# A short-convolution layer in a four-layer backbone step: its weight-pair pool opens earlier, and its last loads are cut by columns

## The chip, the cores and the metric

The kernel runs on one core of a Trainium2 chip. The metric is the device time of one execution in microseconds (us); the times given are medians over runs on the chip. The core has five engines that run side by side, each with its own queue of instructions: PE (TensorE, matrix products), DVE (VectorE), ACT (ScalarE), POOL (GpSimd) and SP (SyncE, which here issues all DMA loads and stores). An engine takes its instructions strictly in order: an instruction that waits holds everything behind it.

## The reference

Four layers work on 640 tokens (512 of a sample, 128 of a prompt) with 1024 channels. Each is `x <- LayerNorm(ALPHA * x + gate * Mixer(x * (1 + scale) + shift))`; shift, scale and gate are computed per layer from a condition vector. The mixers are an HGRN2 recurrence (layer 0), the short convolution (layer 1), an RG-LRU (layer 2) and latent attention (layer 3). The change is in layer 1:

```python
def short_conv_mixer(h, w_in, conv_w, conv_b, w_out):
    bg, cg, v, g = jnp.split(h @ w_in, 4, axis=-1)
    z = depthwise_conv(cg * v, conv_w, conv_b, (SC_KERNEL // 2, SC_KERNEL // 2))
    return (jax.nn.silu(g) * bg * z) @ w_out
x = layer_norm(DEEPNORM_ALPHA * x + gate * out, ln_g[l], ln_b[l])
```

## The kernel before

**Precision.** Each product is made of three: both operands are split into a high part (`wh`, `xh`: a cast) and a low part (`wl`, `xl`: the operand minus its high part), and high by high, high by low and low by high are summed in PSUM. For a weight tile this means a load by SP (`wraw`, 512 KB, L76), a cast on ACT (L80) and a subtraction on DVE (L82). There are three raw buffers and four pairs of split ones (pool `wp`, NW = 4).

**The convolution layer.** `sconv` (L902) computes, for each of eight blocks j of 128 channels, the four products of `h @ w_in`, the three taps of the convolution on ACT and DVE, and the gated result `o`. Block 0 is computed plainly: `mpair` (L265) makes cg and v, `mtile` (L179) makes bg and then g. Blocks 1 to 7 use a scheme with seven half-size products in place of eight: `_prep_pair` (L85) loads two weight blocks at once (`praw`, 1 MB, L93), forms sums of their quarters on DVE in place (L108), and splits each into high and low: `wab` and `s24` into pool `wp`, `wd` and `s13` (`wdh`, `wdl`, `wsh`, `wsl`) into the pool `self.sw`, where `praw` lives as well. Casts are on ACT (L102), low parts on DVE (L105). `spair` (L199) then runs the seven products on PE (L214) into three PSUM banks `psx`, `psy`, `psz`; between products that use the same bank again ACT copies it out (`keep`, L217 to L221). Its other operand, sums of token halves `t1` to `t4` in the pool `tp`, is made once by `token_sums` (L244). `next_w` (L145) prepares weights ahead; a pair is only prepared if `self.sw` exists (L150). Before the change `self.sw` is opened at L916, after `mpair` of block 0 and after `self.zctx.close()` (L914), which frees the tile z that layer 0's output still uses.

**The output projection.** `outproj` (L426) multiplies `o` by `w_out` in three passes over columns: 0 to 255, 256 to 511, 512 to 1023; within a pass it takes five tiles i of 128 tokens. The product of a tile goes to a PSUM bank `pso` (four banks for five tiles; L175 to L177). DVE then frees the bank by `t1 = pso * gateb` (L447), and adds `ALPHA * z` (L453), where z is the layer's input. In layer 1 z comes back from DRAM as the normalised input without scale and offset, so DVE first applies `lng` and `lnb` to the pass's columns (L451):

```python
if l == 1:
    for v, op in ((self.lng, ALU.mult), (self.lnb, ALU.add)):
        nc.vector.tensor_tensor(out=z[:, i, c0:c0 + cw], in0=z[:, i, c0:c0 + cw], in1=v[:, c0:c0 + cw], op=op)
```

z, `lng` and `lnb` are loaded in `build` (L1529 to L1533), the two gate rows (sample and prompt, broadcast over partitions) in `load_bcast` (L390): five loads of z, then `lng`, `lnb`, two gates, 512 KB each. The order of the instructions on each engine is set by a scheduler that estimates times; the program text gives priorities and the order among equals.

Of the kernel before, what the change touches and what calls it, by code (L numbers as in the profile page):

```python
# [9 lines left out]
F32 = mybir.dt.float32  # L10
# [6 lines left out]
P = 128  # L17
D = 1024
# [6 lines left out]
NT = T // P  # L25
# [25 lines left out]
class Kernel:  # L51
# [337 lines left out]

    def load_bcast(self, l):  # L390
        nc, I = self.nc, self.I
        self.gateb = []
        for s in range(2):
            g = self.bp.tile([P, D], F32, name=f"gateb{l}_{s}", tag=f"gateb{s}")
            nc.sync.dma_start(out=g, in_=self.gate_dram[l][s, :].partition_broadcast(P))
            self.gateb.append(g)
        if l == self.NL - 1:
            self.load_affine(l)

# [500 lines left out]
    def sconv(self):  # L900
        nc, tc = self.nc, self.tc
        with ExitStack() as ctx:  # L902
            sp = ctx.enter_context(tc.tile_pool(name="sp", bufs=1))
            for j in range(KT):
                self.rate = 0.0 if j == 0 else 0.45
                if j == 0:
                    cg = sp.tile([P, T], F32, name="ca0", tag="ca0")
                    p = cg
                    pss = self.mpair()
                    for hf in range(2):  # L910
                        c = SPL[hf]
                        nc.scalar.copy(out=cg[:, c], in_=pss[hf][:, 0])
                        nc.vector.tensor_tensor(out=p[:, c], in0=cg[:, c], in1=pss[hf][:, 1], op=ALU.mult)
                    self.zctx.close()  # L914
                    tp = ctx.enter_context(tc.tile_pool(name="tp", bufs=1))
                    self.sw = ctx.enter_context(tc.tile_pool(name="sw", bufs=2))  # L916
                    with tc.high_priority():
                        self.token_sums(tp)
                else:
                    p, v = self.spair(sp, 0)  # L920
                    nc.vector.tensor_tensor(out=p, in0=p, in1=v, op=ALU.mult)
                zz = sp.tile([P, T], F32, name="zz", tag="zz")

                def cw(i):
                    return self.v("sc_conv_w", i * KT + j, 1)
                nc.scalar.activation(out=zz, in_=p, func=AF.Identity, scale=cw(1), bias=self.v("sc_conv_b", j, 1))
                self.taps(zz, p, (-1, 1), (cw(0), cw(2)))
                th = sp.tile([P, T], F32, name="th", tag="th")
                if j == 0:
                    bg = sp.tile([P, T], F32, name="ca1", tag="ca1")  # L930
                    g = sp.tile([P, T], F32, name="cb0", tag="cb")
                    ps = self.mtile()
                    nc.vector.tensor_tensor(out=self.hv(bg), in0=self.hv(zz), in1=ps, op=ALU.mult)
                    ps = self.mtile()
                    nc.scalar.activation(out=self.hv(th), in_=ps, func=AF.Tanh, scale=0.5)
                    nc.vector.scalar_tensor_tensor(out=self.hv(g), in0=self.hv(th), scalar=1.0, in1=ps, op0=ALU.add,
                                                   op1=ALU.mult)
                    nc.vector.scalar_tensor_tensor(out=self.o[:, j, :], in0=g, scalar=0.5, in1=bg, op0=ALU.mult,
                                                   op1=ALU.mult)
                    continue  # L940
                if j == KT - 1:
                    self.split_o(slice(0, 4), slice(0, HALF))
                bg, g = self.spair(sp, 1)
                if j == KT - 1:
                    self.split_o(slice(4, 7), slice(0, HALF))
                for c in (slice(0, HALF), slice(HALF, T)) if j == KT - 1 else (slice(0, T),):
                    nc.vector.tensor_tensor(out=bg[:, c], in0=zz[:, c], in1=bg[:, c], op=ALU.mult)
                    nc.scalar.activation(out=th[:, c], in_=g[:, c], func=AF.Tanh, scale=0.5)
                    nc.vector.scalar_tensor_tensor(out=g[:, c], in0=th[:, c], scalar=1.0, in1=g[:, c], op0=ALU.add,
                                                   op1=ALU.mult)  # L950
                    nc.vector.scalar_tensor_tensor(out=self.o[:, j, c], in0=g[:, c], scalar=0.5, in1=bg[:, c],
                                                   op0=ALU.mult, op1=ALU.mult)
                    if j == KT - 1:
                        self.split_o(slice(7, 8), c)
                        if c.start == 0:
                            self.split_o(slice(0, 7), slice(HALF, T))
            self.sw = None
# [544 lines left out]
    def build(self):  # L1502
        nc, tc, ctx = self.nc, self.tc, self.ctx
        self.setup()
        self.open_x()
        self.o = self.cp.tile([P, KT, T], F32, name="o")
        self.zdram = self.dp.tile([NT, P, D], F32, name="zdram")
        self.zctx = ExitStack()
        wlist = weight_list(self.NL)
        self.weights(wlist)  # L1510
        self.credit, self.rate = -2.0, 0.0
        self.sw = None
        self.pend = None
        self.adaq, self.adafin = [], []
        self.start()
        for l in range(self.NL):
            if l == 0:
                self.adaq = self.ada_units(0, (2,)) + (self.ada_units(1) if self.NL > 1 else [])
            elif l + 1 < self.NL:
                self.adaq = self.ada_units(l + 1)  # L1520
            self.rate = (0.45, 0.4, 0.6, 0.0)[l]
            if l == 0:
                self.hgrn()
                self.open_z()
                for i in range(NT):
                    nc.sync.dma_start(out=self.z[:, i, :], in_=self.I["x_sample"][i * P:(i + 1) * P, :] if i < 4
                                      else self.I["x_prompt"])
            elif l == 1:
                self.sconv()  # L1529
                self.open_z()  # L1530
                for i in range(NT):
                    nc.sync.dma_start(out=self.z[:, i, :], in_=self.zdram[i])
                self.load_affine(0)  # L1533
            elif l == 2:
                self.rglru()
            else:
                self.actx.close()
                self.mla()
                for i in range(NT):
                    nc.sync.dma_start(out=self.z[:, i, :], in_=self.zdram[i])  # L1540
            with ExitStack() as c2:
                self.bp = c2.enter_context(tc.tile_pool(name=f"bp{l}", bufs=1))
                self.load_bcast(l)
                if l + 1 < self.NL:
                    self.flush_ada()
                    self.coeffs(l + 1)
                self.outproj(l)
        self.zctx.close()
        self.close_x()
        self.actx.close()  # L1550
# [127 lines left out]
```

## Time and profile before

| | |
|---|---|
| median of 3 runs | 1472.36 us (1470.63 to 1477.81) |
| the profiled execution | 1473.87 us, of which the instructions span 1472.1 us |
| PE busy | 1416.0 us (96% of the span) |
| DVE, ACT busy | 1085.2 us (74%), 751.0 us (51%) |
| mean granted TensorE clock | 0.99 |
| layer 0's output projection, PE | 447.4 to 507.3 us |
| first products of layer 1's block 0 | from 507.3 us |
| layer 1's output projection, PE | from 732.3 us |

The profile is of one execution. Busy time is what an engine's instructions took; the waits list says how long an engine stood idle and what ended the wait. Start times are microseconds from the start of the span.

### The profile page before, as it was taken

How to read it: one execution, taken by the hardware profiler on the slowest of the kernel's cores; microseconds unless marked ns; L12 is line 12 of the kernel's file. 1: busy time of each engine (PE TensorE's matmuls, PEld its weight loads, DVE VectorE, ACT ScalarE, POOL GpSimd, SP SyncE). 2: the span in 40 equal slices, each digit the busy share in tenths (PEclk: the TensorE clock that was granted, in tenths of full speed). 3: DMA queues.
4: the chain of work that ended last, by engine and by line, in shares of the span. 5: the costliest groups of instructions: out<-in, count | busy, mean ns of one | idle time of the engine just before them, and what ended most of it. 6: DMA issues, size and time to landing. Idle time of an engine off the chain costs nothing.

```text
span 1472.1 us, 26193 instructions
## 1 busy us (share of the span) xinstructions
PE 1416.0 (96%) x10570; PEld 1299.0 (88%) x10570; DVE 1085.2 (74%) x1987; ACT 751.0 (51%) x1350; POOL 86.0 (6%) x194
## 2 busy tenths in 40 slices
PE   6999999999999989999999999999999999999997
PEld 4898989989989889999988989899899888888795
DVE  4777677477567688888787799786656868677777
ACT  2656456356443545455416577622643467566630
POOL 0000000000000100000001011110110200000002
PEclk9999999999999999999999999999999999999999
DMA  9322324223325344443253433443123200001041
GB/s 349 113 80 72 110 80 163 81 90 118 105 84 196 127 142 133 154 145 142 96 207 103 125 128 130 154 145 111 47 78 105 79 19 17 24 30 30 29 144 72
DMA packets 48920, 160.48 MB, mean 109 GB/s; under 512 B 5840, under 2 KB 11040, under 8 KB 47008
## 3 DMA queue, kind: packets, MB, share of 16 engines
q1 hardware_dynamic: 48800, 158.82, 31.9%
q8 instruction: 83, 1.36, 0.4%
q14 instruction: 37, 0.30, 0.1%
HBM read 149.69 MB, written 9.10 MB: 108 GB/s over the span
## 4 chain that ended last, share of the span: by engine, by line
PE 71%; DVE 14%; ACT 8%; DMA 3%; issue 3%; POOL 1%; SPq 0%; POOLq 0%; DVEq 0%; ACTq 0%
PE psmm L195 14%; PE psx L214 7%; PE pso L175 4%; PE pso L177 4%; PE pso L176 4%; PE psz L214 3%; PE poa L1427 3%; PE psmm L1058 2%; DVE wl L82 2%; PE ptp L1414 2%; PE psA L350 2%; PE psy L214 2%; DVE tr L1088 1%; PE psS L175 1%; PE psS L177 1%
## 5 line engine op out<-in xcount | busy, mean ns | idle before, releaser
L80 ACT CAST wh<-wraw 128x1024 fp32r<-128x1024 f32 (+4 forms) x129 | 127.2, 997 | 124.5 <-PE pso L177 68.3
L195 PE MATMUL psmm<-xh,wh 128*128 128x320 f32 x784 | 186.3, 316 | 2.2 <-ACT vt L707 1.7
L195 PE MATMUL psmm<-xh,wl 128*128 128x320 f32 x784 | 181.5, 311 | 0.0
L195 PE MATMUL psmm<-xl,wh 128*128 128x320 f32 x784 | 180.8, 311 | 0.0
L82 DVE TENSOR_TENSOR wl<-wraw,wh 128x1024 fp32r<-128x1024 f32 (+4 forms) x129 | 147.9, 1158 | 28.6 <-ACT wh L80 28.2
L175 PE MATMUL pso<-wh,xh 128*128 128x256 f32 (+1 forms) x464 | 150.2, 325 | 3.4 <-DVE t L447 3.3
L176 PE MATMUL pso<-wl,xh 128*128 128x256 f32 (+1 forms) x464 | 149.3, 322 | 0.0
L177 PE MATMUL pso<-wh,xl 128*128 128x256 f32 (+1 forms) x464 | 149.2, 322 | 0.0
L195 PEld LDWEIGHTS psmm<-xh,wh 128*128 128x128 f32 x784 | 130.9, 189 | 9.9 <-issue 3.5
L195 PEld LDWEIGHTS psmm<-xl,wh 128*128 128x128 f32 x784 | 131.1, 188 | 2.6 <-issue 2.0
L195 PEld LDWEIGHTS psmm<-xh,wl 128*128 128x128 f32 x784 | 131.8, 188 | 0.7 <-issue 0.6
L175 PEld LDWEIGHTS pso<-wh,xh 128*128 128x128 f32 x464 | 87.9, 190 | 10.9 <-DVE t L447 3.5
L177 PEld LDWEIGHTS pso<-wh,xl 128*128 128x128 f32 x464 | 88.0, 190 | 7.3
L176 PEld LDWEIGHTS pso<-wl,xh 128*128 128x128 f32 x464 | 88.2, 190 | 6.6
L1398 ACT ACTIVATE pe<-psS,mx 128x768 f32<-128x768 f32 (+1 forms) x80 | 63.7, 797 | 38.8 <-DVE mx L1396 38.4
L1396 DVE TENSOR_REDUCE mx<-psS 128x1 f32<-128x768 f32 (+1 forms) x80 | 65.3, 817 | 7.8 <-PE psS L177 7.1
L1414 PE MATMUL ptp<-ident,pe 128*128 128x128 f32 x400 | 56.8, 273 | 0.8 <-ACT pe L1398 0.8
L447 DVE TENSOR_TENSOR t<-pso,gateb 128x256 f32<-128x256 f32 (+1 forms) x58 | 29.2, 510 | 31.3 <-PE pso L177 30.1
L177 PE MATMUL psmm<-xh,wl 128*128 128x384 f32 (+1 forms) x160 | 49.4, 308 | 1.1 <-DVE wl L82 1.1
L176 PE MATMUL psmm<-xl,wh 128*128 128x384 f32 (+1 forms) x160 | 49.9, 312 | 0.3 <-DVE xl L166 0.3
L175 PE MATMUL psmm<-xh,wh 128*128 128x384 f32 (+1 forms) x160 | 49.8, 311 | 0.0
L1427 PE MATMUL poa<-pT,v 128*64 128x256 f32 (+1 forms) x416 | 48.8, 377 | 0.7 <-ACT pT L1416 0.4
(497 smaller groups left out, 3786.1 us busy)
## 6 DMA issues: line engine op xcount, KB each, us to landing
wraw<-in_wpack SPq DMA_DIRECT2D x109, 512.0 KB
araw<-in_ada_rest SPq DMA_DIRECT2D x80, 512.0 KB
praw<-in_wpack SPq DMA_DIRECT2D x14, 1024.0 KB
araw<-in_ada_first SPq DMA_DIRECT2D x16, 512.0 KB
zdram<-z SPq DMA_DIRECT2D x10, 512.0 KB
z<-zdram SPq DMA_DIRECT2D x10, 512.0 KB
gateb<-gate_dram SPq DMA_DIRECT2D x8, 512.0 KB
wraw<-in_wpack SPq DMA_DIRECT2D x8, 320.0 KB
```

The lines of the kernel that those rows point to most:

```text
L80: self.tc.keep_in_program_order(nc.scalar.copy(out=wh[:, :n], in_=raw[:, :n]))
L82: nc.vector.tensor_tensor(out=wl[:, :n], in0=raw[:, :n], in1=wh[:, :n].bitcast(F32), op=ALU.subtract)
L175: nc.tensor.matmul(ps, lhsT=ah, rhs=bh, start=(i == 0), stop=False)
L176: nc.tensor.matmul(ps, lhsT=ah, rhs=bl, start=False, stop=False)
L177: nc.tensor.matmul(ps, lhsT=al, rhs=bh, start=False, stop=(i == n - 1))
L195: nc.tensor.matmul(ps[hf][:, :HALF], lhsT=w[:, k, :], rhs=x[:, k, hf * HALF:(hf + 1) * HALF], start=(first and k == 0), stop=(last and k = ...
L214: nc.tensor.matmul(ps, lhsT=u[:, k, :], rhs=v[:, k, :], start=(first and st and k == 0), stop=(en and k == 3), skip_group_check=True)
L350: nc.tensor.matmul(ps[32 * j:32 * j + 32, :], lhsT=self.csil[:, k, :], rhs=raw[:, j * 256:(j + 1) * 256], start=(k == 2 * u), stop=(k == 2 ...
L1396: nc.vector.reduce_max(out=mx, in_=ps[:, :nk], axis=AX.X, negate=True)
L1398: nc.scalar.activation(out=pe[:, :nk], in_=ps[:, :nk], func=AF.Exp, bias=mx[:, 0:1], accum_out=g["sm"][:, n, hp:hp + 1])
L1414: nc.tensor.transpose(pt[:, kk, :], pe[:, (k0 + kk) * P:(k0 + kk + 1) * P], self.ident)
L1427: nc.tensor.matmul(po[hp * 64:(hp + 1) * 64, 0, :nq], lhsT=v4[:, kt, vc + hp * 64:vc + (hp + 1) * 64], rhs=g["pt"][hp][:, kk, :nq], start= ...
```

## The change

Two edits. In `sconv` the pool `self.sw` is opened together with `sp`, before block 0, and no longer after `tp`. At the end of layer 1, z, `lng`, `lnb` and the gates are loaded by the columns of the three passes: eighteen loads of 128 KB to 768 KB in place of nine of 512 KB, all in `load_bcast` now. The bytes are the same.

```diff
     def load_bcast(self, l):
         nc, I = self.nc, self.I
-        self.gateb = []
-        for s in range(2):
-            g = self.bp.tile([P, D], F32, name=f"gateb{l}_{s}", tag=f"gateb{s}")
-            nc.sync.dma_start(out=g, in_=self.gate_dram[l][s, :].partition_broadcast(P))
-            self.gateb.append(g)
+        self.gateb = [self.bp.tile([P, D], F32, name=f"gateb{l}_{s}", tag=f"gateb{s}") for s in range(2)]
+        for c in (slice(0, 256), slice(256, 512), slice(512, D)) if l == 1 else (slice(0, D),):
+            if l == 1:
+                nc.sync.dma_start(out=self.z[:, 0:2, c], in_=self.zdram[0:2, :, c].rearrange("i p n -> p i n"))
+                if c.start == 0:
+                    self.lng = self.zp.tile([P, D], F32, name="lng0", tag="lng")
+                    self.lnb = self.zp.tile([P, D], F32, name="lnb0", tag="lnb")
+                nc.sync.dma_start(out=self.lng[:, c], in_=I["ln_g"][0, c].partition_broadcast(P))
+                nc.sync.dma_start(out=self.lnb[:, c], in_=I["ln_b"][0, c].partition_broadcast(P))
+            for s in range(2):
+                nc.sync.dma_start(out=self.gateb[s][:, c], in_=self.gate_dram[l][s, c].partition_broadcast(P))
+                if l == 1 and s == 0:
+                    nc.sync.dma_start(out=self.z[:, 2:NT, c], in_=self.zdram[2:NT, :, c].rearrange("i p n -> p i n"))
         if l == self.NL - 1:
             self.load_affine(l)
...
     def sconv(self):
...
             sp = ctx.enter_context(tc.tile_pool(name="sp", bufs=1))
+            self.sw = ctx.enter_context(tc.tile_pool(name="sw", bufs=2))
             for j in range(KT):
...
                     self.zctx.close()
                     tp = ctx.enter_context(tc.tile_pool(name="tp", bufs=1))
-                    self.sw = ctx.enter_context(tc.tile_pool(name="sw", bufs=2))
...
             elif l == 1:
                 self.sconv()
                 self.open_z()
-                for i in range(NT):
-                    nc.sync.dma_start(out=self.z[:, i, :], in_=self.zdram[i])
-                self.load_affine(0)
```

The changed file is longer, so the same statement has a higher line number in it: L447, L451, L453, L455 become L456, L460, L462, L464, and L913 becomes L923. A number behind a name is a buffer; `pso_1_3` is the third index of the second pass, token tile 3.

**Place 1, layer 0's output projection, second pass.** SP's queue before; `wraw_5244` to `wraw_5407` are the four weight tiles of the third pass, `wraw_5413` and `wraw_5419` those of `mpair`:

```order
L76 DMA wraw_5244<-in_wpack 128x1024
L344 DMA arows_6132<-in_ada_b 1x256 x2
L76 DMA wraw_5250<-in_wpack 128x1024
L76 DMA wraw_5401<-in_wpack 128x1024
L344 DMA arows_6132<-in_ada_b 1x256
L76 DMA wraw_5407<-in_wpack 128x1024
L344 DMA arows_6132<-in_ada_b 1x256
L76 DMA wraw_5413<-in_wpack 128x1024
```

And now:

```order
L76 DMA wraw_5244<-in_wpack 128x1024
L93 DMA praw_5871<-in_wpack 128x2048
L76 DMA wraw_5250<-in_wpack 128x1024
L76 DMA wraw_5401<-in_wpack 128x1024
L76 DMA wraw_5407<-in_wpack 128x1024
L93 DMA praw_5998<-in_wpack 128x2048
L76 DMA wraw_5413<-in_wpack 128x1024
```

The first two pair loads stand here now; before they stood sixteen rows further down, behind all five of layer 0's stores of z. On DVE the work of both pairs comes along as far as it needs no `wp` buffer. Before, from the end of the same pass:

```order
L455 BN_STATS stats_5086<-z 128x6
L82 TENSOR_TENSOR wl_5403<-wraw_5401,wh_5402 128x1024
L447 TENSOR_TENSOR t_5397<-pso_1_4_5372,gateb_1_5042 128x256
L82 TENSOR_TENSOR wl_5409<-wraw_5407,wh_5408 128x1024
L453 SCALAR_TENSOR_TENSOR z<-z,t_5397 128x256
```

And now (the second pair, `praw_5998`; the first pair's four stand further up in the same way):

```order
L105 TENSOR_TENSOR wdl_6003<-praw_5998,wdh_6002 128x512
L456 TENSOR_TENSOR t_5368<-pso_1_3_5343,gateb_0_5040 128x256
L108 TENSOR_TENSOR praw_5998<-praw_5998 128x512
L462 SCALAR_TENSOR_TENSOR z<-z,t_5368 128x256
L108 TENSOR_TENSOR praw_5998<-praw_5998 128x512
L464 BN_STATS stats_5086<-z 128x6
L82 TENSOR_TENSOR wl_5403<-wraw_5401,wh_5402 128x1024
L105 TENSOR_TENSOR wsl_6005<-praw_5998,wsh_6004 128x1024
L82 TENSOR_TENSOR wl_5409<-wraw_5407,wh_5408 128x1024
L456 TENSOR_TENSOR t_5397<-pso_1_4_5372,gateb_1_5041 128x256
```

Four pieces per pair (`wdl`, two sums, `wsl`) have moved here; one of them stands between two low parts that the third pass needs.

**Place 2, the start of layer 1.** DVE before, from the first low part of a pair on:

```order
L105 TENSOR_TENSOR wl_5874<-praw_5871,wh_5873 128x1024
L105 TENSOR_TENSOR wdl_5876<-praw_5871,wdh_5875 128x512
L105 TENSOR_TENSOR wdl_6003<-praw_5998,wdh_6002 128x512
L166 TENSOR_TENSOR t2l<-o,t2h 128x1280
L108 TENSOR_TENSOR praw_5871<-praw_5871 128x512
L108 TENSOR_TENSOR praw_5998<-praw_5998 128x512
L108 TENSOR_TENSOR praw_5871<-praw_5871 128x512
L108 TENSOR_TENSOR praw_5998<-praw_5998 128x512
L166 TENSOR_TENSOR t3l<-o,t3h 128x1280
L261 SCALAR_TENSOR_TENSOR o<-o 128x4x320
```

And now:

```order
L105 TENSOR_TENSOR wl_5874<-praw_5871,wh_5873 128x1024
L166 TENSOR_TENSOR t3l<-o,t3h 128x1280
L166 TENSOR_TENSOR t2l<-o,t2h 128x1280
L108 TENSOR_TENSOR praw_5871<-praw_5871 128x512
L261 SCALAR_TENSOR_TENSOR o<-o 128x4x320
L108 TENSOR_TENSOR praw_5871<-praw_5871 128x512
L923 TENSOR_TENSOR ca_5700<-ca_5700,psmm 128x256
L166 TENSOR_TENSOR t4l<-o,t4h 128x1280
```

On PE the second `mtile` of block 0 (`psmm`, 48 products) stood behind the products of `psy` and `psz` with pair weights; now it stands ahead of most of them, and the first pair's products follow one another like this:

```order
L214 MATMUL psx<-xh,wl_5874 128x320
L214 MATMUL psz<-t1h,wsl_5878 128x320
L214 MATMUL psz<-t1h,wsh_5877 128x320
L214 MATMUL psz<-t1l,wsh_5877 128x320
L214 MATMUL psz<-t1h,wsl_5878 128x320
L350 MATMUL psA_0_0_6134<-araw_0_0_6135,csil 32x256
L214 MATMUL psx<-t2h,wh_5879 128x320
```

Only these five stand between the end of one product in `psx` and the next one in it.

**Place 3, the start of layer 1's output projection.** DVE before, `wl_8077` being the second low part of the first pass:

```order
L166 TENSOR_TENSOR xl<-o,xh 128x320
L82 TENSOR_TENSOR wl_8077<-wraw_8075,wh_8076 128x1024
L82 TENSOR_TENSOR wl_8083<-wraw_8081,wh_8082 128x1024
L82 TENSOR_TENSOR wl_8089<-wraw_8087,wh_8088 128x1024
L451 TENSOR_TENSOR z<-z,lng_8053 128x256 x5
L451 TENSOR_TENSOR z<-z,lnb_8055 128x256 x5
L447 TENSOR_TENSOR t_8118<-pso_0_0_8093,gateb_0_8060 128x256
```

And now:

```order
L166 TENSOR_TENSOR xl<-o,xh 128x320
L460 TENSOR_TENSOR z<-z,lng_8054 128x256 x2
L82 TENSOR_TENSOR wl_8086<-wraw_8084,wh_8085 128x1024
L82 TENSOR_TENSOR wl_8092<-wraw_8090,wh_8091 128x1024
L82 TENSOR_TENSOR wl_8098<-wraw_8096,wh_8097 128x1024
L456 TENSOR_TENSOR t_8127<-pso_0_0_8102,gateb_0_8051 128x256
L460 TENSOR_TENSOR z<-z,lnb_8055 128x256
```

The first `t` has come up to directly behind the three low parts, but two products with `lng` now stand ahead of them.

## Rows read from the trace of the kernel before

**Rows 1.** The page, busy time of each engine, share and instructions.
```profile
PE 1416.0 (96%) x10570; PEld 1299.0 (88%) x10570; DVE 1085.2 (74%) x1987; ACT 751.0 (51%) x1350; POOL 86.0 (6%) x194
```

**Rows 2.** PE's waits: what it waited for, us, times, longest.
```profile
PE psy L214 <- ACT wh L102: 3.8, 1, 3.8
...
PE pso L175 <- DVE t L447: 3.3, 1, 3.3
```

**Rows 3.** Windows at the first wait: PE busy (instructions), clock, DMA share, GB/s.
```profile
533.04:536.80 3.76, 0.00 (x0) 0.89 0.78 264
536.80:542.72 5.92, 5.92 (x21) 0.50 0.28 68
```

**Rows 4.** Windows at the second wait, columns as in Rows 3.
```profile
744.07:747.51 3.44, 0.16 (x2) 1.00 1.02 416
747.51:751.03 3.52, 3.52 (x17) 0.52 0.72 291
```

**Rows 5.** Chain of waits from 505 to 560 us: start, us, what.
```profile
515.01 7.15 DMA praw<-in_wpack
...
528.68 2.41 DVE praw L108 x4
531.09 1.40 DVE t3l L166
...
533.93 1.26 ACT t4h L163
535.19 1.57 ACT wh L102 x3
...
544.40 7.04 PE psmm L195 x48
```

**Rows 6.** Windows: PE, PEld, DVE, ACT, POOL busy, clock, DMA share, GB/s.
```profile
462.00:477.00 15.00, 15.00 (x124) 14.82 (x124) 10.02 (x21) 3.00 (x3) 0.00 (x0) 1.00 0.39 137
515.00:541.00 26.00, 21.90 (x152) 20.62 (x151) 25.04 (x30) 14.19 (x23) 0.00 (x0) 0.90 0.45 162
```

**Rows 7.** DVE's timeline from 735 us: start, us, what [idle before, releaser].
```profile
736.30 3.50 DVE L82 TENSOR_TENSOR wl<-wraw,wh 128x1024 fp32r<-128x1024 f32 x3 [0.46 <-ACT wh L80]
743.13 1.77 DVE L451 TENSOR_TENSOR z<-z,lng 128x256 f32<-128x256 f32 x5 [3.33 <-DMA lng<-in_ln_g]
745.36 1.77 DVE L451 TENSOR_TENSOR z<-z,lnb 128x256 f32<-128x256 f32 x5 [0.46 <-DMA lnb<-in_ln_b]
```

**Rows 8.** SP's timeline at 732 us: issues of z's loads.
```profile
732.50 2.26 SPq L1532 DMA_DIRECT2D z<-zdram  x5
```

**Rows 9.** DVE's and PE's timelines at the start of layer 1.
```profile
523.77 1.22 DVE L105 TENSOR_TENSOR wl<-praw,wh 128x1024 fp32r<-128x1024 f32 x1
...
529.82 0.31 PE L214 MATMUL psy<-xh,wh 128*128 128x320 f32 x1
```

**Rows 10.** Timelines of PE and ACT: a bank's last product and its copy.
```profile
715.07 0.31 PE L214 MATMUL psx<-t3h,wsl 128*128 128x320 f32 x1
715.47 0.43 ACT L220 COPY u<-psx 128x320 f32<-128x320 f32 x1 [1.39 <-PE psx L214]
```

**Rows 11.** Tile praw: durations in ns, least, median, most; first and last start.
```profile
L105 DVE TENSOR_TENSOR wsl<-praw,wsh x14: 1214/1218/1220, 536.8 to 711.2; 128x1024 fp32r<-128x1024 f32 x14
```

**Rows 12.** Timelines of SP, DVE and PE in layer 0's output projection.
```profile
460.64 1.82 SPq L76 DMA_DIRECT2D wraw<-in_wpack  x2
465.91 1.22 DVE L82 TENSOR_TENSOR wl<-wraw,wh 128x1024 fp32r<-128x1024 f32 x1 [0.75 <-ACT wh L80]
477.24 1.21 DVE L82 TENSOR_TENSOR wl<-wraw,wh 128x1024 fp32r<-128x1024 f32 x1
477.30 0.40 PE L175 MATMUL pso<-wh,xh 128*128 128x512 f32 x1
```

**Rows 13.** Timelines of SP and ACT: a weight load's issue and its first use.
```profile
453.20 1.30 SPq L76 DMA_DIRECT2D wraw<-in_wpack  x3
456.81 1.05 ACT L80 CAST wh<-wraw 128x1024 fp32r<-128x1024 f32 x1 [4.04 <-DMA wraw<-in_wpack]
```

## The prediction

> **What bounds the kernel now.** I read the page first: PE is busy for 1416.0 us, 96% of the span, so the end moves only by what PE stands idle or runs slowly [rows 1]. Next come PE's waits. In the part of the program that the change touches there are two, one each: 3.8 us in `psy`, for a cast of a pair's weights, and 3.3 us in `pso`, for DVE's `t` [rows 2].
>
> Then the clock around each, because a wait can cost more than its length. After the first, PE works from 536.80 to 542.72 at a granted clock of 0.50, which is 1.2 GHz in place of 2.4: 21 products take 5.92 us [rows 3]. The second leaves 3.52 us at 0.52 [rows 4]. Before both, PE had been idle for over three microseconds. The Trainium skill's page "TensorE: Matmul & The Clock Gate", section "Part 1: The HAM clock gate", describes this fall to half rate, but advises leaving its ramp out of a model, since it is below one percent of a typical span.
>
> Then who is late. At the first wait the chain runs from the load of the first two pairs, issued only at 515.01, over DVE's sums and ACT's `t4h` to three casts at 535.19 [rows 5]. DVE is busy for 25.04 of the 26 us from 515 to 541, PE for 21.90 [rows 6]. DVE is full here; in the second and third pass of layer 0's output before it (462 to 477) it has 15 - 10.02 = 5.0 us free, and ACT 12 us.
>
> At the second wait DVE stands idle for 3.33 us until `lng` lands at 743.1, multiplies five tiles, waits again for `lnb` and adds five more; only then, at about 745.4 + 1.7 = 747.1, comes the first `t`, which frees the bank that PE wants [rows 7]. The first load of z was issued at 732.50 [rows 8]. DMA moved 416 GB/s at the end of this stretch [rows 4]: the loads are limited by their bytes, and DVE waits for columns that the first pass does not need.
>
> **The change part by part.** *First wait, what goes.* Idle 3.77 us (533.03 to 536.80), and of the 5.92 us at half clock 0.50 x 5.92 = 2.96 us: together 6.7 us. Two things remove it. The second `mtile`, 7.04 us of PE work [rows 5], now stands ahead of the products that wait, and that alone is more than 3.77. And DVE's two `wdl` and four sums have left the chain: six times 2.41/4 = 0.60, that is 3.6 us [rows 5], of which one sum comes back in front of `o` (0.6).
>
> What could be late next: `mtile` needs a PSUM bank that `ca` (now L923) frees. From the low part at 523.77 DVE now takes this (1.22), three pieces of 1280 columns (1.40 each), two sums (0.60) and `ca`, a fifth of such a piece (0.28) [rows 5, 9]: 523.77 + 6.9 = 530.7. PE came to `psy` at 529.82 [rows 9] and does eight products at 7.04/48 = 0.147 first, so it asks at 531.0. A margin of 0.3 us: bounds 0 and 1 us (the error of so many terms), and I take 0.
>
> *The copies of* `psx`. Five products now stand between two uses of the bank, 5 x 0.147 = 0.7 us. A bank's last product starts at 715.07, its copy ends at 715.90: 0.83, less 0.15 for the product itself, 0.7 us [rows 10]. If a weight cast of 1.57/3 = 0.52 stands ahead of the copy on ACT, PE waits about 0.5; one does ahead of the first. Bounds 0 and three times 0.5; I take 0.4.
>
> *Layer 0's output.* Per pair `wdl` and two sums (0.60 each) and `wsl`, 1.22 [rows 11], come in: 6.0 us for both, against 5.0 free, so something slides by about 1 us. The banks cover `t`. The tight place is the low part that began at 477.24 and ended at 478.45, ahead of which a `wsl` (1.22) has been put, while a `t` of 256 columns (0.28 by its size) went behind. PE uses that low part 12 products after 477.30; a product of 320 columns takes 0.147 (the 48 of `mtile`), one of 512 thus 0.235, so at 480.1 [rows 5, 12]: of 1.65 us 0.7 are left. Bounds 0 and 0.7; I take 0. ACT's six casts (3.1 us) fit into 12 us. The pair loads add 2.1 MB to SP's queue; at 416 GB/s 2.5 us each, in a stretch that moves 137 GB/s [rows 6].
>
> *Second wait, what goes.* 3.28 us idle and 0.48 x 3.52 = 1.69 at low clock [rows 4]: 5.0 us. Now the first `t` needs only the first pass's columns.
>
> *Second wait, what comes.* Two products with `lng` stand ahead of the low part that PE needs at once. A 512 KB load was issued at 453.20 and used at 456.81 [rows 13]: 3.6 us, of which 1.26 are bytes at 416 GB/s, so about 2.35 are fixed. The first z piece and `lng`, 384 KB, issued at 732.50 and 0.45 later, land at 732.95 + 2.35 + 0.9 = 736.2. The two products take 2 x 1.77/5 = 0.7, the low parts start at 736.9 in place of 736.30: 0.6 late [rows 7, 8]. Bounds 0 and, if the pieces arrive as late as the whole tile did (743.1), 7.5; the fixed part of rows 13 is nearest, and I take 0.5. The first `t` then comes at 736.9 + 3.5 = 740.4, where PE asks at 744.07 + 0.5: 4 us of margin.
>
> *Sum.* 6.7 + 5.0 - 0.4 - 0.5 = 10.8 us less. The profiled execution took 1473.87, 1.5 above the median, so 1463.1 for it; for the median 1472.36 - 10.8 = 1461.6. By the page's advice, with the waits alone, it would be 7.05 - 0.9 = 6.2 us less, 1466.2.
>
> **The rivals.** *One wait comes back in another place.* At the end: `lng` lands 3 us or more late and DVE holds the low parts, which no PSUM banks cushion; PE then waits as long as before and loses the clock again. Gain 6.7 - 0.4 = 6.3, 1466.1. At the start: the `ca` chain or a copy is late by 3 us; gain 5.0 - 0.5 = 4.5, 1467.9. For it: DVE's order is strict, the margins are 0.3 and nothing. Against: half of DVE's excess has gone, and the loads are the same kind as before.
>
> *The clock's part is not given back.* PE waits less, but small waits remain in both places and it still runs them at 1.2 GHz: 1466.2. Against: both falls came within one idle stretch of over 3 us, and those stretches go. [...]
>
> *Slower: SP is held.* The first `praw` load now stands ahead of three weight tiles of layer 0's third pass. If its memory is not free when SP reaches it, those tiles wait behind it. The next tile was issued at 460.64, its low part ended at 467.1 and PE used it at 477.30 [rows 12]: 10.2 us of cover. PE stalls by the time beyond 470.8, and the kernel is slower once the hold passes 470.8 + 10.8 = 481.6. Held as long as in the old pool, to 515.01 [rows 5], it would be 44 us of stall: 1472 - 11 + 44 = 1505. For it: that load did go out as late as 515.01. Against: the pool is now opened below what layer 0 still uses, and its first load no longer stands behind the stores of z.
>
> *No change.* Both waits go, and other waits of the same size appear behind them: 1472. DVE, full from 515 on, would have to stay late.
>
> **How the numbers follow.** Forecast 0.70; one wait back 0.14; clock not given back 0.05; no change 0.07; slower 0.04. The forecast's own range is 1459 to 1465: the unknown costs at zero (11.7 less) and the lowest run, 1.7 below the median, at one end; at the other 3.4 us of them more. For 8 in 10 the range takes in the cases up to 1468: 1459 to 1468. A measurement of this kernel can tell about 0.5%, 7.4 us, from no change: faster means below 1465.0. That is the forecast, 0.70; within 0.5% lie one wait back, the clock and no change, 0.26; slower 0.04.
>
> **What would show it.** In the changed kernel's profile the two lines of PE's waits are gone, and PE's granted clock is 1.00 from 505 to 770 us. DVE's `wsl` of the first two pairs stand before 480 us. `lng` lands within 4 us of z's first issue, and the first `t` of layer 1 comes before PE has filled four banks. It is wrong if PE waits over 1 us for `wl` at the first pass, for `ca` or a copy at the second `mtile` and the first pair, or if SP issues the third pass's weights of layer 0 later than 470 us.

## The result and the profile after

The changed kernel takes 1464.11 us (median of 5 runs, 1461.02 to 1465.82) against 1474.52 for the kernel before in the same comparison: a ratio of 0.9929, interval [0.9913, 0.9946], or 10.4 us less. The forecast was 1461.6, 10.8 us less. Most of what is left between 1461.6 and 1464.11 is the base: the forecast stood on a median of 1472.36, and more runs of the kernel before gave 1474.5 to 1475.2.

PE's waits in the changed kernel, from 447 us to 832 (the whole of what the change touches):

```profile
PE psA L350 <- DMA araw<-in_ada_rest: 1.2, 2, 1.0
PE pso L176 <- DVE wl L82: 1.1, 1, 1.1
PE psmm L176 <- DVE xl L166: 0.3, 1, 0.3
```

Both rows of [rows 2] are gone. `psA` and `psmm` waited before too (1.4 and 0.3 us there). New is 1.1 us for `wl`. The clock, in windows (columns as in Rows 6):

```profile
505.00:770.00 265.00, 263.45 (x1893) 249.40 (x1892) 217.13 (x349) 124.03 (x225) 3.43 (x7) 1.00 0.42 146
```

PE is busy for 263.45 of 265 us, at 1.00 all the way; before, two stretches of it ran at half clock [rows 3, 4].

Where the time came from is read by stage, between first products of the output projections. The tile `pso` before, in layer 0's (first row) and layer 1's projection, with first and last start at the end of the times:

```profile
L175 PE MATMUL pso<-wh,xh x120: 277/284/483, 447.4 to 505.8; 128*128 128x256 f32 x80, 128*128 128x512 f32 x40
L177 PE MATMUL pso<-wh,xl x120: 277/285/415, 732.5 to 796.5; 128*128 128x256 f32 x80, 128*128 128x512 f32 x40
```

And in the changed kernel:

```profile
L175 PE MATMUL pso<-wh,xh x120: 277/285/482, 450.1 to 508.5; 128*128 128x256 f32 x80, 128*128 128x512 f32 x40
L177 PE MATMUL pso<-wh,xl x120: 277/285/396, 728.3 to 788.5; 128*128 128x256 f32 x80, 128*128 128x512 f32 x40
```

The first products of L175 in layer 1 started at 732.3 and 728.0. So three stages, in us:

| stage | before | after | difference |
|---|---|---|---|
| start of the program to layer 0's output projection | 447.4 | 450.1 | +2.7 |
| from there to layer 1's output projection (first wait) | 284.9 | 277.9 | -7.0 |
| layer 1's output projection, first to last product (second wait) | 64.3 | 60.5 | -3.8 |
| the whole span | 1472.1 | 1463.9 | -8.2 |

The rest of the span differs by 0.1. The first stage holds the same instructions in both kernels; its 2.7 us are scatter between executions: added up from the clock in the traces, PE stood at half clock for 13.7 us of it before and for 20.5 us after (last section). The two stages that the change touches give 10.8 us.

The places that the forecast named, in the changed kernel. SP's queue in layer 0's output projection:

```profile
456.75 0.33 SPq L93 DMA_DIRECT2D praw<-in_wpack  x1
463.36 3.59 SPq L76 DMA_DIRECT2D wraw<-in_wpack  x3
```

The first pair load left at 456.75, and the weight tiles behind it at 463.36, 2.7 later than before [rows 12], which is the 2.7 of the first stage: SP was not held. DVE there and at the start of layer 1:

```profile
471.39 1.22 DVE L105 TENSOR_TENSOR wsl<-praw,wsh 128x1024 fp32r<-128x1024 f32 x1
...
479.66 1.22 DVE L105 TENSOR_TENSOR wsl<-praw,wsh 128x1024 fp32r<-128x1024 f32 x1
...
533.03 0.42 DVE L923 TENSOR_TENSOR ca<-ca,psmm 128x256 f32<-128x256 f32 x1
```

And PE's chain of work at that second place:

```profile
525.66 7.04 PE psmm L195 x48
532.70 1.17 PE psy L214 x8
533.87 7.04 PE psmm L195 x48
```

The second `mtile` started at 533.87 without a wait; `ca`, which frees its bank, had ended at 533.45. The start of layer 1's output projection, in the timelines of SP and DVE:

```profile
728.22 0.39 SPq L396 DMA_DIRECT2D z<-zdram  x1
728.65 0.47 SPq L400 DMA_DIRECT2D lng<-in_ln_g  x1
```

```profile
732.80 0.76 DVE L460 TENSOR_TENSOR z<-z,lng 128x256 f32<-128x256 f32 x2 [1.20 <-DMA lng<-in_ln_g]
733.48 3.49 DVE L82 TENSOR_TENSOR wl<-wraw,wh 128x1024 fp32r<-128x1024 f32 x3
736.88 0.41 DVE L456 TENSOR_TENSOR t<-pso,gateb 128x256 f32<-128x256 f32 x1
```

The first `t` came at 736.9, as forecast right behind the low parts. But DVE stood 1.20 us for `lng` and then multiplied two tiles of z before the first low part could start, at 733.48. That is PE's new wait.

### The profile page after: what moved, and what is told of

The parts are those of the page before. It is cut to its first block, busy times and chain, and to the rows that moved or that the text cites. A ratio compares the mean times of both kernels' runs of the same rounds, so it can differ in the third digit from the quotient of the medians.

```text
span 1463.9 us, 26209 instructions
## 1 busy us (share of the span) xinstructions
PE 1415.1 (97%) x10570; PEld 1298.0 (89%) x10570; DVE 1084.8 (74%) x1987; ACT 751.4 (51%) x1350; POOL 87.0 (6%) x194
## 4 chain that ended last, share of the span: by engine, by line
PE 73%; DVE 13%; ACT 8%; issue 3%; DMA 2%; POOL 1%; SPq 0%; POOLq 0%; DVEq 0%; ACTq 0%
PE psmm L195 14%; PE psx L214 7%; PE pso L176 4%; PE pso L177 4%; PE pso L175 4%; PE psz L214 3%; PE poa L1436 3%; PE psmm L1067 2%; DVE wl L82 2%; PE ptp L1423 2%; PE psA L350 2%; PE psy L214 2%; DVE tr L1097 1%; PE psS L175 1%; PE psS L177 1%
## 5 line engine op out<-in xcount | busy, mean ns | idle before, releaser
L175 PE MATMUL pso<-wh,xh 128*128 128x256 f32 (+1 forms) x464 | 149.4, 323 | 0.1
L175 PEld LDWEIGHTS pso<-wh,xh 128*128 128x128 f32 x464 | 87.2, 188 | 7.4 <-ACT xh L163 0.4
L175 PE MATMUL psmm<-xh,wh 128*128 128x384 f32 (+1 forms) x160 | 49.9, 312 | 0.0
L1423 PEld LDWEIGHTS ptp<-ident,pe 128*128 128x128 f32 x400 | 46.4, 140 | 2.4 <-ACT pe L1407 1.1
```

What stands on the lines that cost most here:

```text
L175: nc.tensor.matmul(ps, lhsT=ah, rhs=bh, start=(i == 0), stop=False)
L1423: nc.tensor.transpose(pt[:, kk, :], pe[:, (k0 + kk) * P:(k0 + kk + 1) * P], self.ident)
```

## The experiments

Times are compared with runs of the kernel before on the same chip: 1475.16 us (24 runs) for the first four, 1475.10 (11) for the next four, 1474.80 (11) for the last four. "Between the projections" is from the first `pso` product of layer 0 to that of layer 1 (284.9 before); "the projection" is layer 1's, first to last product (64.3 before).

### One edit at a time

The first edit alone (`e1_pool_only`):

```diff
             sp = ctx.enter_context(tc.tile_pool(name="sp", bufs=1))
+            self.sw = ctx.enter_context(tc.tile_pool(name="sw", bufs=2))
...
-                    self.sw = ctx.enter_context(tc.tile_pool(name="sw", bufs=2))
```

> The first edit alone: the pool of the pairs' weights opens with the layer, the loads at the layer's end stay nine whole ones. Theory: the two waits are independent, and each is worth its own idle time and its own stretch at half clock. From the first product of layer 0's output projection to that of layer 1's it takes 277.9 us as with both edits (284.9 before); in pso the 3.3 us for t stay, with a granted clock near 0.5 behind them; 1474.5 - 7.0 = 1467.5 us. Rival: layer 1 is bound by DVE over its whole length, and what the start gains is lost by its end: some 284 us between the two projections, 1474 us.

The second alone (`e2_columns_only`) is the diff of the change without these two lines.

> The second edit alone: z, scale, offset and gates of layer 1's end in eighteen loads by columns, the pool opens where it did. Theory of independent waits: psy keeps its wait of 3.8 us and 21 products at 0.50; at the end PE waits 1.1 us for wl in place of 3.3 for t, and the clock stays at 1.00, so that from layer 1's output projection to layer 2's first product with uh it takes 95.5 us (99.3 before); 1474.5 - 3.9 = 1470.6 us. Rival: with both edits the end gained since layer 1 came 4 us earlier against the loads; alone the end gives nothing, 1474.5 us, or the low parts wait for lng by more than 3 us.

Measured: 1469.74 us, ratio 0.9965 [0.9953, 0.9977], and 1470.84 us, ratio 0.9971 [0.9959, 0.9984]: 5.2 and 4.3 us by the ratios, together 9.5 where both edits gave 10.5 by theirs. Each edit works where it stands. With the first alone it is 277.9 us between the projections and 64.5 for the projection, with the wait for `t` as before:

```profile
PE pso L175 <- DVE t L447: 3.7, 1, 3.7
```

With the second alone the projection takes 60.5, and PE's two waits are

```profile
PE psy L214 <- ACT wh L102: 2.7, 1, 2.7
PE pso L176 <- DVE wl L82: 1.1, 1, 1.1
```

The rivals (the gain is lost again by layer 1's end; the end alone gains nothing) fall. One thing was not expected. The start of layer 1 is the old one in `e2_columns_only`, yet `psy` waited 2.7 us there and not 3.8, and it took 282.7 between the projections, not 284.9. So the first wait's price differs between executions, from 4.8 (282.7 - 277.9) to 7.0 us. The ratio of `e1_pool_only` gives 5.2, between the two.

The traces show what differed. The loads of the first two pairs were issued 67.6 us after layer 0's first `pso` product in both, but ACT stood longer for them before. The first cast of a pair's weights, and the casts that end PE's wait, in the kernel before:

```profile
522.38 1.14 ACT L102 CAST wh<-praw 128x512 fp32r<-128x512 f32 x2 [1.90 <-DMA praw<-in_wpack]
...
535.10 2.17 ACT L102 CAST wh<-praw 128x512 fp32r<-128x512 f32 x4
```

And in `e2_columns_only`:

```profile
523.20 1.14 ACT L102 CAST wh<-praw 128x512 fp32r<-128x512 f32 x2 [0.27 <-DMA praw<-in_wpack]
...
536.46 2.17 ACT L102 CAST wh<-praw 128x512 fp32r<-128x512 f32 x4
```

From that first product (447.4 and 449.85) it is 75.0 us to the first cast before and 73.4 here, 87.7 and 86.6 to the others. The wait is 1.1 us shorter because the load landed earlier, and behind it 11 products ran at half clock in place of 21.

### Which half of the first edit

The edit does two things at once: PE's second `mtile` moves ahead, and four pieces per pair leave DVE's full stretch. Each was tried alone. `e3_ca_early` changes the kernel before by one priority:

```diff
-                        nc.scalar.copy(out=cg[:, c], in_=pss[hf][:, 0])
-                        nc.vector.tensor_tensor(out=p[:, c], in0=cg[:, c], in1=pss[hf][:, 1], op=ALU.mult)
+                        with tc.high_priority():
+                            nc.scalar.copy(out=cg[:, c], in_=pss[hf][:, 0])
+                            nc.vector.tensor_tensor(out=p[:, c], in0=cg[:, c], in1=pss[hf][:, 1], op=ALU.mult)
```

> The kernel before with one thing moved: the copy and the product that make ca have high priority, so the product stands 18 rows further up on DVE and the second mtile of block 0 directly behind the first on PE. All the pairs' work on DVE and ACT stays where it was. Theory: the wait of 3.8 us went because 7.0 us of ready products now stand ahead of the ones that waited, so this alone removes it and the 3 us at half clock: 278 to 279 us between the two output projections, 1467 to 1468 us. Rival: DVE's six moved pieces, 3.6 us, are what removed it; with DVE still full from 515 on, PE waits 2 us or more for wl, wh or a copy a little later, and the time is 1471 to 1475 us.

`e7_mtile_late` has the pool early, and the second `mtile` written behind the first `spair` of block 1:

```diff
                     p, v = self.spair(sp, 0)
+                    if j == 1:
+                        rest0()
...
-                    ps = self.mtile()
...
+                    gw = self.next_w()
+
+                    def rest0(th=th, g=g, bg=bg):
+                        ps = self.mtile(w=gw)
...
```

> The first edit alone, but the second mtile of block 0 is written behind the first half of block 1, so that PE takes it as late as before; the four early pieces of each pair on DVE stay early. Theory: each half of the first edit is enough by itself; the pair's chain is 3 us shorter, so PE waits at most 1 us there, the clock stays at 1.00: 278 to 279 us between the two output projections, 1475.2 - 6 = 1469 us. Rival: only PE's order did it; the chain is as late as before, PE waits 2.5 us or more for wh, wl or ca, and half clock follows: 282 to 285 us, 1473 to 1475 us.

Measured: 1470.01 us, ratio 0.9968 [0.9956, 0.9979], and 1469.43 us, ratio 0.9955 [0.9943, 0.9967]. Neither waits for the pair's weights any more, and both run this part at full clock. PE at the start of layer 1 in `e3_ca_early` (520 to 560, columns as in Rows 6) and in `e7_mtile_late`:

```profile
520.00:560.00 40.00, 40.00 (x282) 38.04 (x281) 33.01 (x41) 18.72 (x30) 0.00 (x0) 1.00 0.37 133
```

```profile
505.00:560.00 55.00, 54.66 (x372) 52.17 (x372) 48.66 (x64) 31.73 (x57) 1.10 (x2) 1.00 0.38 134
```

278.9 us between the projections in the first, 277.8 in the second. Either half is enough; "only PE's order" and "only DVE's relief" are both wrong. In `e7_mtile_late` the pairs' loads come early too; they were not tried apart from DVE's pieces. The 1.0 us more of the first lies in no single wait: its products of `psA`, `psy` and `psz` start a little further apart. In time it gave 4.7 us by its ratio, less than the 6.5 to 7.5 expected.

### The clock's part

`e4_fill` takes away no wait. It puts work for PE into one:

```diff
         p1 = keep(x, "p1")
+        if self.fill and n == 1:
+            self.fill = False
+            for k in range(26):
+                nc.tensor.matmul(y, lhsT=self.xh[:, k % 4, 0:P], rhs=self.xh[:, k % 4, N1], start=True, stop=True,
+                                 skip_group_check=True)
```

> The kernel before with 26 extra products into the bank psy, 26 x 0.147 = 3.8 us, ahead of the ones that waited; their result is overwritten by the first of these. Nothing that is waited for comes earlier. Theory: of the 6.7 us half is the clock, which falls because PE stood idle; with PE kept busy the 21 products behind run at 1.00 and take 3.0 in place of 5.9 us: 281.9 us between the two output projections, 1474.5 - 3.0 = 1471.5 us. Rival: the low clock has another cause than the idle time and stays, or the extra products only add to the path: 285 to 289 us, 1474.5 to 1478 us.

Measured: 1471.56 us, ratio 0.9984 [0.9974, 0.9993], 282.3 us between the projections. The 26 extra products, then the 21 that follow:

```profile
532.47:536.50 4.03, 4.03 (x31) 4.03 (x28) 4.03 (x6) 3.15 (x5) 0.00 (x0) 1.00 0.77 260
536.50:539.50 3.00, 3.00 (x21) 2.81 (x20) 3.00 (x3) 0.43 (x1) 0.00 (x0) 1.00 0.00 0
```

21 products take 3.0 us at 1.00, where [rows 3] has 5.92 at 0.50. With PE kept busy the clock did not fall: half clock was a price of its own, and here idle time was its cause.

What that is worth cannot be read from 284.9 - 282.3 = 2.6, because the load landed early in this profile, as in `e2_columns_only`. The casts began 86.6 us after layer 0's first product (446.84) and not 87.7:

```profile
533.45 2.18 ACT L102 CAST wh<-praw 128x512 fp32r<-128x512 f32 x4
```

So the extra products held PE 1.2 us longer than the weights did (`psy` went on after 89.5 us, after 88.3 in `e2_columns_only`). That run, with the same casts and no fill, paid for its wait with

```profile
538.17:541.39 3.22, 3.22 (x11) 3.03 (x12) 3.22 (x4) 0.47 (x1) 0.00 (x0) 0.50 0.35 144
```

which is 1.6 us of clock; less the 1.2 us, 0.4 is left, and 282.7 - 282.3 is 0.4. Over all runs the gain in time is 2.4 us by the ratio (1.0 to 3.8). Work that computes nothing paid for itself, but by how much depends on when the load lands.

### The new wait at the end

`e5_low_first` keeps the low parts ahead of the first product with `lng`:

```diff
+            low = nc.vector.tensor_tensor(out=wl[:, :n], in0=raw[:, :n], in1=wh[:, :n].bitcast(F32), op=ALU.subtract)
+        if self.lowfirst:
+            self.tc.keep_in_program_order(low)
...
+                        if q == 0 and v is self.lng:
+                            tc.keep_in_program_order(za)
+                            self.lowfirst = False
```

> Both edits, and on DVE the three low parts of the first pass are kept ahead of the first product of z with lng; nothing else differs. Theory: the 1.1 us that PE waits for wl in the changed kernel are DVE standing for lng (1.20 us) and the two products with it (0.7 us); the casts end at 732.0, so without them the first low part is there at 733.2, when PE asks for it at 733.6. The wait goes, t comes in time (it needs only the gate): 94.4 us from layer 1's output projection to layer 2's first product with uh (95.5 with both edits), 1.1 us less than the changed kernel, 1463.0 us on the scale on which that took 1464.1. Rival: the low parts are late for their casts or the next wait takes its place (t or a later wl): 95.5 us, no gain.

`e8_gate_first` puts `lng` later instead: gate, `lnb`, two tiles of z, `lng`, three tiles of z, second gate.

> Both edits, with the first chunk in another order: gate, lnb, two tiles of z, then lng, and the rest. One product with lng still stands on DVE ahead of the low parts, and lng now comes fourth. Theory: what the second edit gives hangs on when lng lands; issued 1 us later behind 256 KB more it lands 1 to 1.5 us later, PE's wait for wl grows from 1.1 to between 1.4 and 2.3 us, since one product less stands there: 95.8 to 96.7 us from layer 1's output projection to layer 2's first product, if the clock stays at 1.00; up to 1.7 us more if it falls. 1464.5 to 1467 us. Rival: lng lands no later, since these loads wait for nothing but their own latency: 95.1 us, 0.3 us less than with both edits.

Measured: 1461.21 us, ratio 0.9909 [0.9894, 0.9923], and 1463.58 us, ratio 0.9914 [0.9902, 0.9927]. DVE in `e5_low_first`:

```profile
727.97 3.49 DVE L82 TENSOR_TENSOR wl<-wraw,wh 128x1024 fp32r<-128x1024 f32 x3 [0.46 <-ACT wh L80]
731.38 0.41 DVE L458 TENSOR_TENSOR t<-pso,gateb 128x256 f32<-128x256 f32 x1
731.72 0.41 DVE L462 TENSOR_TENSOR z<-z,lng 128x256 f32<-128x256 f32 x1
```

DVE stands for the cast alone now, 0.46 us, as before the change. PE waits neither for `wl` nor for `t`, and the projection takes 59.2 us, 1.3 less than with both edits. To layer 2's first product with `uh` only 0.3 of it was left in this profile (95.2 us, not 94.4): the waits for `araw` that follow were 2.3 us here and 1.2 in the changed kernel. That is scatter of those loads: the same kernel measured again (`e10_low_first_again`) waited 1.3 us for them and took 94.5. In `e8_gate_first`:

```profile
731.98 0.43 DVE L460 TENSOR_TENSOR z<-z,lng 128x256 f32<-128x256 f32 x1 [1.76 <-DMA lng<-in_ln_g]
```

DVE stood 1.76 us for `lng` in place of 1.20, so it did land later, by about half of the 1 to 1.5 us expected; one product less stood there, and PE waited 1.2 us, less than the 1.4 expected. To layer 2's first product with `uh` it took 96.3 us, within the 95.8 to 96.7 expected, but the time cannot tell it from the changed kernel. That the wait hangs on `lng` is shown by `e5_low_first`; this run moves it by 0.1 us only, the right way.

### Order or cut

`e6_whole_reordered` has the first edit and nine whole loads, in another order:

```diff
-        for c in (slice(0, 256), slice(256, 512), slice(512, D)) if l == 1 else (slice(0, D),):
...
+        nc.sync.dma_start(out=self.gateb[0], in_=self.gate_dram[l][0, :].partition_broadcast(P))
+        if l == 1:
+            nc.sync.dma_start(out=self.z[:, 0, :], in_=self.zdram[0])
+            self.load_affine(0)
+            for i in range(1, 4):
+                nc.sync.dma_start(out=self.z[:, i, :], in_=self.zdram[i])
+        nc.sync.dma_start(out=self.gateb[1], in_=self.gate_dram[l][1, :].partition_broadcast(P))
+        if l == 1:
+            nc.sync.dma_start(out=self.z[:, 4, :], in_=self.zdram[4])
```

> The first edit, and in place of the second one the nine whole loads of before in another order: gate of the sample, first tile of z, lng, lnb, three tiles of z, gate of the prompt, last tile of z. On DVE the first t then stands directly behind the three low parts and no product with lng ahead of them. Theory: the wait in pso was 3.3 us because seven whole loads stood ahead of the gate and ten products ahead of the first t; the order is what counts, not the cut. The gate lands about 4 us after its issue, t comes at once, PE waits for neither t nor wl: 94.4 us from layer 1's output projection to layer 2's first product, 1 us less than the changed kernel, 1463 us. Rival: the first pass needs its columns of everything early, and whole tiles bring twice to four times the bytes; DVE stands for z and lnb (five loads, 2.5 MB, 6.3 us at 416 GB/s) and PE waits 1 to 3 us for t: 96 to 99 us, 1465 to 1468 us.

Measured: 1461.85 us, ratio 0.9907 [0.9892, 0.9922]. DVE:

```profile
733.16 3.50 DVE L82 TENSOR_TENSOR wl<-wraw,wh 128x1024 fp32r<-128x1024 f32 x3 [0.46 <-ACT wh L80]
736.57 0.42 DVE L452 TENSOR_TENSOR t<-pso,gateb 128x256 f32<-128x256 f32 x1
736.91 0.41 DVE L456 TENSOR_TENSOR z<-z,lng 128x256 f32<-128x256 f32 x1
```

No wait for `t` or `wl`, 59.2 us for the projection, 94.5 to the first product with `uh`. The cut by columns is not needed: an order of whole loads that brings the gate first, with `t` ahead of the products with `lng` on DVE, is enough. Which of the two counts more was not tried apart.

### Once more, side by side

> The changed kernel once more, beside the next two. Layer 1's output projection, from its first product to its last, 60.5 us as in the first profile (64.3 before), one wait of 1.1 us for wl; 1464 us, a ratio of 0.992 to 0.994 to the kernel before.

> The low parts ahead of the products with lng, once more. Theory: 59.2 us for layer 1's output projection, no wait for wl, 1.3 us less than the changed kernel beside it. Rival: the difference in time of the first measurement, 0.2%, was scatter, and the 1.3 us are lost again by layer 2's first product (loads of araw): the same time within 0.5 us.

> The first edit with nine whole loads in the new order, once more. Theory (order, not cut): 59.2 us for layer 1's output projection, no wait for t or wl; 1 to 1.5 us less than the changed kernel beside it. Rival: whole tiles leave no margin, and in another execution PE waits for t: 60.5 us or more.

`e12_priority_and_order` is `e3_ca_early` with the loads of `e6_whole_reordered`; the pool stays where it was.

> The kernel before, with the pool where it was and whole loads: only the copy and product that make ca have high priority, and the nine loads come in the order of the run with whole loads. Theory: PE's two waits go for two reasons, ready products ahead of the first and the loads that the first t needs ahead of the others; neither the early pool nor the cut by columns is needed. 278.9 us between the two output projections, as with ca alone, 59.2 us for layer 1's; 1 us more than the run with whole loads, 1463 us where that takes 1462. Rival: with DVE full to the end of layer 1's start and no early loads, a wait of 1 us or more comes back: 1465 to 1469 us.

| run | us (6 runs) | ratio | between the projections | the projection |
|---|---|---|---|---|
| e9_both_again | 1464.16 | 0.9930 [0.9917, 0.9942] | 277.9 | 60.5 |
| e10_low_first_again | 1462.32 | 0.9917 [0.9900, 0.9933] | 278.0 | 59.4 |
| e11_whole_again | 1463.03 | 0.9919 [0.9905, 0.9934] | 278.0 | 59.2 |
| e12_priority_and_order | 1464.73 | 0.9933 [0.9920, 0.9945] | 279.6 | 59.2 |

By the profile the low parts first and the whole loads reordered save 1.1 to 1.3 us of the changed kernel's projection, in both profiles of each. In time they are 1.8 and 1.1 us below it here, but the intervals overlap: ahead of the kernel before for certain, ahead of the changed one only by what the profile shows. `e12_priority_and_order` has neither edit of the change and reaches the changed kernel's time within 0.6 us; it took 0.7 us more between the projections than expected, and in time 1.7 us more than `e11_whole_again`, where 1 was expected.

## Why the prediction was right

- **First wait, 6.7 us less 0.4 for copies:** 7.0 us by the profile. The 3.77 idle and the 2.96 of half clock went, as worked out. The 0.4 for ACT's copies of `psx` did not come. Both reasons given hold, each by itself (`e3_ca_early`, `e7_mtile_late`). What the step did not see is that this price is that of one execution, in which the first pair's load landed late: in another the same wait cost 4.8.
- **Margins at the start:** `ca` ended 0.4 us before PE asked for its bank, where 0.3 had been worked out.
- **Layer 0's output, taken at nothing:** no wait of PE there, though two `wsl`, two `wdl` and four sums were added. Cover was DVE's and ACT's free time [rows 6] and it held. (The window from 462 to 477 us is the second pass alone; the third begins at 477.30 [rows 12].)
- **Second wait, 5.0 us less 0.5:** the projection gained 3.8, not 4.5. The term that was too small is the one for `lng` ahead of the low parts, 0.5 against a wait of 1.1. The step took the fixed part of a 512 KB load [rows 13] and bytes at 416 GB/s, and had `lng` land 3.7 us after the first issue of z; it took 4.45 (issue at 728.65, 4.02 us to landing, by the chain of waits below), beyond the 4 us that the text had set as its own sign. PE's 1.1 us for `wl` also meets, just, the first of the signs that it had set for being wrong (over 1 us).

```profile
728.65 4.02 DMA lng<-in_ln_g
733.14 0.42 DVE z L460
733.56 1.14 DVE wl L82
734.74 0.39 PE pso L176
```

- **The cause named for the second wait** was half right. DVE waited for columns that the first pass did not need, as was said; but a `t` needs only the gate, and putting the nine loads and the ten products on DVE in another order is enough to bring it in time, with loads of the old size (`e6_whole_reordered`).
- **Sum:** 10.8 us forecast; 10.8 in the two stages of the profile, 10.4 by medians. That it fits so closely is partly luck: +0.7 at the start and -0.7 at the end cancel. Both 10.8 also take the first wait from the same execution of the kernel before; with the load as in `e2_columns_only` it would be 2.2 us less.
- **Rivals.** One wait coming back: 1.1 us did, a third of the size at which that rival counted it, and the clock stayed at 1.00. Clock not given back: excluded by the window from 505 to 770, and by `e4_fill` from the other side. The advice of the Trainium skill's page "TensorE: Matmul & The Clock Gate", section "Part 1: The HAM clock gate", not to fit the ramp in a model is given there for the start of a kernel; carried over to these two waits, as the prediction did, it gives 6.2 us, outside the interval (0.9913 to 0.9946 of 1474.5 is 8.0 to 12.8 us). SP held: not at all. No change: excluded.

## What to carry to other kernels

A wait of the engine that bounds the kernel costs its idle time and, where the clock falls, more behind it: in these profiles half of 2.9 to 6.1 us at half clock, 0.4 to 0.8 of the idle time. Both go if ready work that has to be done anyway stands in the gap, so look first for a product that could be ordered there (here one priority did nearly as much as an early pool). Before cutting loads into pieces, ask what the first consumer needs and put that load first; and do not let an instruction that waits for a DMA be placed ahead of one that the bounding engine needs next.

## What was not expected of the hardware

**The same wait has more than one price.** After `pso`'s wait PE ran 2.9 us at half clock in `e1_pool_only` (3.70 idle), 3.4 before and in `e3_ca_early` (3.28 and 3.32 idle; [rows 4]), 5.6 in `e4_fill` (3.53 idle) and 6.1 in `e7_mtile_late` (3.97 idle); it does not follow the length of the wait. The five kernels have the same instructions there. In windows, `e1_pool_only`, `e4_fill` and `e7_mtile_late`:

```profile
744.33:747.24 2.91, 2.91 (x13) 2.91 (x14) 2.91 (x10) 0.00 (x0) 0.00 (x0) 0.50 0.81 325
```

```profile
744.64:750.22 5.58, 5.58 (x26) 5.58 (x27) 5.44 (x15) 1.10 (x2) 0.00 (x0) 0.50 0.43 171
```

```profile
742.01:748.08 6.07, 6.07 (x28) 6.07 (x29) 5.81 (x15) 1.59 (x2) 0.00 (x0) 0.50 0.35 140
```

After the wait of 1.10 us for `wl` the clock stayed at 1.00.

**Such stretches come and go in code that nobody touched.** From the start to layer 0's output projection the 14 profiles took between 446.0 and 451.2 us, with the same instructions. The stretch from 354.36 to 357.77 us, in the kernel before and in the changed one:

```profile
354.36:357.77 3.41, 3.41 (x31) 3.41 (x31) 3.41 (x6) 3.38 (x6) 0.00 (x0) 1.00 0.43 136
```

```profile
354.36:357.77 3.41, 3.41 (x18) 3.41 (x17) 3.41 (x8) 3.37 (x5) 0.00 (x0) 0.50 0.13 31
```

PE is busy throughout in both, but at half clock it does 18 products in place of 31. Added up over this part of the program, PE stood at half clock for 10.2 us in the profile that took 446.0 us and for 23.9 us in the one that took 451.2. That is a part of the scatter of several us between runs, and a reason to read a gain of this size by stage.

**Loads by columns moved fewer bytes at a full queue, for most of the time.** A piece of 256 columns is 1 KB in a row, a whole row 4 KB. The loads of the changed kernel, then those of the kernel before:

```profile
734.00:736.00 2.00, 1.26 (x10) 1.26 (x11) 2.00 (x3) 0.00 (x0) 0.00 (x0) 1.00 1.01 315
```

```profile
738.00:740.00 2.00, 2.00 (x19) 2.00 (x18) 1.80 (x2) 0.17 (x1) 0.00 (x0) 1.00 1.02 412
```

At the same busy share it is 315 GB/s against 412. The whole rows have a slow stretch too, so the length of a row is not shown to be the only cause:

```profile
740.00:742.00 2.00, 2.00 (x19) 2.00 (x19) 0.00 (x0) 0.00 (x0) 0.00 (x0) 1.00 1.06 305
```

Why `lng` came later than worked out with 416 stays open. At 315 GB/s the 384 KB of the first piece of z and of `lng` would take 0.3 us longer, where 0.75 are missing, and just before it landed at 732.67 the queue of the changed kernel was not full:

```profile
730.00:732.00 2.00, 1.97 (x17) 1.76 (x15) 1.07 (x3) 1.39 (x3) 0.00 (x0) 1.00 0.81 137
```
